# A decoder trunk in f32: the opening's products reordered, and one chunk with P3 ahead of P6

## The chip, the cores and the metric

The kernel runs on one core of a Trainium2 chip. The metric is the device time of one execution in microseconds. Engines are named as in the profile: PE is TensorE (PEld its weight loads), DVE is VectorE, ACT is ScalarE, POOL is GpSimd and SP is SyncE. POOL and SP issue the loads here.

## The reference

The input x has 512 tokens of width 1024 in float32. The trunk has two layers. Each is a half-weighted SwiGLU feed-forward part, a token mixer, and a second feed-forward part; all three read a normed h.

```python
def swiglu(x, w_in, w_out):
    g, u = jnp.split(x @ w_in, 2, axis=-1)
    return (jax.nn.silu(g) * u) @ w_out

for i in range(2):
    h = h + 0.5 * swiglu(rms_norm(h, ffn1_norm[i]), ffn1_w_in[i], ffn1_w_out[i])   # D_FF = 2816
    h = h + mixer_i(rms_norm(h, mix_norm[i]))     # layer 0: RG-LRU, layer 1: spatial gating
    h = h + 0.5 * swiglu(rms_norm(h, ffn2_norm[i]), ffn2_w_in[i], ffn2_w_out[i])
return rms_norm(h, final_norm)
```

The change touches only the start of the first feed-forward part.

## The kernel before

**Products in three parts.** Every f32 operand is split into a rounded hi part and the rest, lo. A product is three matmuls: hi by hi, hi by lo, lo by hi. For a weight tile ("raw", 512 KB) ScalarE writes whi and VectorE writes wlo; activations get hi and lo in the same way (`split`, `Group.parts`). There are four buffers each for whi and wlo, so a split waits until PE is through with the sub-step four places back. There are eight raw buffers.

**Sub-steps.** The program is one list, `subs`. A sub-step is twelve matmuls on one weight tile. The loop at the end of the kernel walks the list; in each turn it runs hooks of the phases pre, mid, rest, end and late, splits the weights of sub-steps up to three places ahead (`SPLIT_AHEAD`; the first turns have their own numbers in `ahead`), issues loads while a raw buffer is free, and writes the sub-step's products. Each engine carries out its instructions in the order in which this loop writes them. So an instruction that waits holds up all that is behind it on its engine.

**The opening.** The first 256 columns of the feed-forward part (`pair_plain`, `first=True`) are computed by plain blocks. The normed x is taken as quarters A11, A12, A22, A21 (tokens in halves by columns in halves); each quarter is loaded, transposed by PE, copied out of PSUM with the norm's gain, and split. The list is: A12 by two tiles; A11 and S1 by two tiles, S1 = A21 - A22 being multiplied by the tile that A11 has just used; and A22 by two tiles, for which VectorE adds the A12 tile to the A11 tile. The transposes stand behind the first two steps. The row scale `rt` (from squares, a root and a Newton step) is applied after the product, as the gate activation's scale.

**A chunk.** All other parts of x @ w_in and the output products use seven block products in place of eight (`seven`). For one chunk each of the seven, P1, P2, P5, P6, P3, P7, Q4 in this order, is two sub-steps (groups 0 and 1 of the inner dimension). The left sides are given by `LEFT`: P6 uses S2, P3 uses S4. The right sides come out of few tiles:

- P5 uses tile 11 after VectorE has added tile 12 to it (`Sub.add`). Then POOL issues an accumulating load that adds block 22 to tile 12, which P7 will use.
- P6 uses tile 11 after VectorE has added tile 22 to it; then an accumulating load adds block 21 to tile 11, which Q4 will use.
- P3 uses tile 22 as it was loaded.

**Banks.** `BANK` says where a product is summed. P1 starts bank A, P2 bank B, P5 bank C. P6, P7 and Q4 add to A, and P3 adds to C. Each intermediate sum is read out before the next product is added: in `chunk` a function per product does this, for the two token tiles s. `p5` copies C to c5 on ScalarE. `p6` copies A to c2, and `p3` subtracts that copy from C and multiplies by the gate c1: the result c is transposed by PE (`left_blocks`, line 260) at the end of P7's first step. A product that adds to a bank waits until the bank's last read-out is done.

Lines in the profile: L87 is every VectorE tensor_tensor, L96 every ScalarE activation, L260 the transposes, L345 to L347 a chunk's matmuls, L692 to L694 those of the opening, L136 the accumulating loads.

Of the kernel before, what the change touches and what calls it, by code (L numbers as in the profile page):

```python
# [10 lines left out]
AF = mybir.ActivationFunctionType  # L11
ALU = mybir.AluOpType

P = 128
D = 1024
T = 512
H = T // 2
# [26 lines left out]


ORDER = ("P1", "P2", "P5", "P6", "P3", "P7", "Q4")
LEFT = {"P1": "A11", "P2": "A12", "P5": "S1", "P6": "S2", "P3": "S4", "P7": "S3", "Q4": "A22"}
BANK = {"P1": ("A", True), "P2": ("B", True), "P5": ("C", True), "P6": ("A", False), "P3": ("C", False),
        "P7": ("A", False), "Q4": ("A", False)}
# [3 lines left out]
def trunk(ctx: ExitStack, tc: tile.TileContext, a: dict, out: bass.AP):  # L53
# [41 lines left out]
    def act(o, x, f, **k):  # L95
        nc.scalar.activation(out=o, in_=x, func=f, **k)  # L96
# [218 lines left out]
            return [p[:, o : o + P] for p in g.hl[LEFT[prod]]]  # L315
        return left

    def seven(block, cuts, left, w, posts, order=None, own=False, apart=False, joined=None):

        bk, raw, held = {}, {}, []
        banks = dict(BANK, Q4=("Q", True)) if apart else BANK

        def mm_of(prod, ci):
            name, fresh = banks[prod]
            pairs = cuts[ci]

            def mm(sub):
                if fresh and ci == 0:
                    for s in range(2):
                        bk[name, s] = bank(name)[:, :w]
                if prod == joined and ci == 0:
                    held.extend((sub, q, i) for q, i in enumerate(pairs))
                    return
                for s in range(2):
                    ps = bk[name, s]
                    k = {} if fresh else dict(skip_group_check=True)  # L340
                    for sb, q, i in (held if prod == joined else []) + [(sub, q, i) for q, i in enumerate(pairs)]:
                        zh, zl = left(prod, i, s)
                        wh, wl = sb.hi[:, q, :], sb.lo[:, q, :]
                        end = i == cuts[-1][-1]
                        nc.tensor.matmul(ps, zh, wh, start=fresh and i == 0, stop=False, **k)  # L345
                        nc.tensor.matmul(ps, zl, wh, start=False, stop=False, **k)  # L346
                        nc.tensor.matmul(ps, zh, wl, start=False, stop=end, **k)  # L347
# [273 lines left out]
        return left_of(lambda: S.z)  # L621


    def chunk(w_in, f0, nt, group):

        w = nt * P
        c1, c2, c3, c5, ht = {}, {}, {}, {}, {}
# [4 lines left out]
        def new(d, s, name):  # L632
            d[s] = slot(name=name)[:, :w]
            return d[s]
# [25 lines left out]
        def q4(s, ps):  # L660
# [4 lines left out]
            if s == 1:  # L665
                left_blocks(group, ht, 1)

        seven(in_block(w_in, lambda n: n * DFF + f0 * P, w), [[0, 1], [2, 3]], x_left(), w,
              dict(P1=p1, P2=p2, P5=p5, P6=p6, P3=p3, P7=p7, Q4=q4))

    def pair_plain(w_in, f0, group, first=False):

# [10 lines left out]
                st[half, s] = bank("p")  # L683
            return st[half, s]

        def product(sub, half, left, h, start, stop):
            for s in range(2):
                ps = bank_of(half, s)
                for q in range(2):
                    zh, zl = (p[:, q * H + s * P : q * H + (s + 1) * P] for p in S.z[h].hl[left])  # L690
                    wh, wl = sub.hi[:, q, :], sub.lo[:, q, :]
                    nc.tensor.matmul(ps, zh, wh, start=start and q == 0, stop=False)  # L692
                    nc.tensor.matmul(ps, zl, wh, start=False, stop=False)  # L693
                    nc.tensor.matmul(ps, zh, wl, start=False, stop=stop and q == 1)  # L694

        def post(half):
            for s in range(2):
# [5 lines left out]
            left_blocks(group, ht, half, 3 if first and half else 2)  # L703

        for h in range(2):
            subs.append(Sub(raw[1, h], lambda sub, h=h: product(sub, 0, "A12", h, h == 0, False)))
        for h in range(2):
            subs.append(Sub(raw[0, h], lambda sub, h=h: (product(sub, 0, "A11", h, False, h == 1),
                                                         product(sub, 1, "S1", h, h == 0, False)),
                            None if h == 0 else (lambda: hook(now[0] + 1, "rest", lambda: post(0))) if first else  # L710
                            lambda: post(0)))
# [553 lines left out]
    def load_more(n=len(raws)):  # L1265
        nonlocal loaded
        while loaded < n and len(live) < RAW_BUFS:
            raws[loaded].load()
            loaded += 1

    raws[0].halves = True
    load_x(0, 512, 256)
    load_x(0, 768, 256)
    load_more(2)
    load_x(0, 0)
    load_x(2, 512)
    load_x(2, 0)
    load_more()
# [34 lines left out]
        if parts:  # L1313
            first.g[i].parts("S1" if name == "A21" else name)

    opening = {}
    def take_plain(i, name):

        g, ps = first.g[i], opening.pop((i, name))
        t = g.new(name)  # L1320
        for q, gain in enumerate(first.src(i, name)[1]):
            qs = slice(q * H, (q + 1) * H)
            ts(t[:, qs], ps[:, qs], gain, None, ALU.mult)

    turn(0, "A12")
    warm_up(2, 512)
# [27 lines left out]
    hook(100, "rest", lambda: list(consts))  # L1354
    ahead = {0: 1, 1: 3, 2: 4, 3: 6}

    for i, s in enumerate(subs):
        now[0] = i
# [1 line left out]
        run("pre")  # L1360
        upto = ahead.get(i, i + SPLIT_AHEAD)
        for q in range(i, min(upto + 1, len(subs))):
            if i >= 2 and q == upto and q + 1 < len(subs):
                subs[q + 1].add()
            subs[q].split()
        run("mid")
# [33 lines left out]
```

## Time and profile before

| | |
|---|---|
| median of 3 runs | 1653.03 us (1652.65 to 1653.19) |
| profiled execution | 1654.62 us, span 1652.9 us |
| PE busy | 1624.5 us (98%) |
| DVE, ACT, POOL busy | 1373.8 (83%), 1034.6 (63%), 210.5 us (13%) |
| granted TensorE clock, mean | 0.993 |
| loads on POOL's queue | 86.06 MB, 31.1% of 16 engines' span |
| loads on SP's queue | 181.95 MB, 36.0% |

A line of the timeline has the start, the duration (of one instruction, or of a run of xN), engine, line, operation, output and inputs, shape, count and, in brackets, the engine's idle time just before and what ended it. Buffer numbers are left out of names: A, B, C are banks, whi and wlo a weight's parts, hi and lo an activation's, raw a loaded tile, e a transposed block, s in the first 80 us mostly S1. A row of the stretches has the busy time of each engine with its count, then the granted clock, the DMA engines' share, and GB/s.

### The profile page before, as it was taken

How to read it: one execution, taken by the hardware profiler on the slowest of the kernel's cores; microseconds unless marked ns; L12 is line 12 of the kernel's file. 1: busy time of each engine (PE TensorE's matmuls, PEld its weight loads, DVE VectorE, ACT ScalarE, POOL GpSimd, SP SyncE). 2: the span in 40 equal slices, each digit the busy share in tenths (PEclk: the TensorE clock that was granted, in tenths of full speed). 3: DMA queues.
4: the chain of work that ended last, by engine and by line, in shares of the span. 5: the costliest groups of instructions: out<-in, count | busy, mean ns of one | idle time of the engine just before them, and what ended most of it. 6: DMA issues, size and time to landing. Idle time of an engine off the chain costs nothing.

```text
span 1652.9 us, 20807 instructions
## 1 busy us (share of the span) xinstructions
PE 1624.5 (98%) x7475; PEld 1336.9 (81%) x7475; DVE 1373.8 (83%) x1825; ACT 1034.6 (63%) x1487; POOL 210.5 (13%) x191
## 2 busy tenths in 40 slices
PE   8999999989999999999999999999999999999996
PEld 6788888878878888888888888888888888888885
DVE  5898897786798897887988978878966988879777
ACT  6656656666867656556676565566874765665655
POOL 1111111200010111111101111111200011121110
PEclk9999999999999999999999999999999999999998
DMA  6767876952463866976838778768863557696683
GB/s 205 158 174 175 208 165 153 218 140 77 102 148 92 195 164 162 217 182 155 203 96 182 173 163 208 185 161 202 218 172 90 151 119 188 166 209 168 157 206 77
DMA packets 160744, 271.97 MB, mean 165 GB/s; under 512 B 11280, under 2 KB 37504, under 8 KB 160640
## 3 DMA queue, kind: packets, MB, share of 16 engines
q1 hardware_dynamic: 113424, 181.95, 36.0%
q0 software_dynamic: 44992, 86.06, 31.1%
q10 hardware_dynamic: 2224, 2.63, 0.5%
q8 instruction: 59, 0.97, 0.2%
q14 instruction: 45, 0.37, 0.1%
HBM read 268.50 MB, written 2.10 MB: 164 GB/s over the span
## 4 chain that ended last, share of the span: by engine, by line
PE 86%; DVE 8%; ACT 4%; issue 2%; DMA 1%; SPq 0%; ACTq 0%; DVEq 0%
PE A L346 13%; PE A L347 13%; PE A L345 13%; PE C L346 7%; PE C L347 7%; PE C L345 7%; PE B L345 3%; PE B L347 3%; PE B L346 3%; PE e L260 3%; DVE wlo L87 2%; PE p L694 1%; PE p L692 1%; PE p L693 1%; PE Q L347 1%
## 5 line engine op out<-in xcount | busy, mean ns | idle before, releaser
L96 ACT ACTIVATE whi<-raw 128x1024 fp32r<-128x1024 f32 (+1 forms) x539 | 556.4, 1034 | 421.4 <-PE A L346 107.4
L87 DVE TENSOR_TENSOR wlo<-raw,whi 128x1024 fp32r<-128x1024 f32 (+1 forms) x539 | 640.5, 1191 | 198.3 <-ACT whi L96 197.4
L345 PE MATMUL A<-whi,hi 128*128 128x512 f32 x984 | 393.0, 399 | 0.0
L346 PE MATMUL A<-whi,lo 128*128 128x512 f32 x984 | 385.5, 392 | 2.5 <-DVE lo L87 2.4
L347 PE MATMUL A<-wlo,hi 128*128 128x512 f32 x984 | 385.5, 392 | 0.2 <-DVE wlo L87 0.2
L346 PEld LDWEIGHTS A<-whi,lo 128*128 128x128 f32 x984 | 185.8, 189 | 41.7 <-DVE lo L87 4.8
L347 PEld LDWEIGHTS A<-wlo,hi 128*128 128x128 f32 x984 | 185.4, 188 | 40.8 <-DVE wlo L87 0.6
L345 PEld LDWEIGHTS A<-whi,hi 128*128 128x128 f32 x984 | 185.7, 189 | 36.5
L346 PE MATMUL C<-whi,lo 128*128 128x512 f32 x544 | 212.4, 390 | 0.9 <-DVE lo L87 0.7
L345 PE MATMUL C<-whi,hi 128*128 128x512 f32 x544 | 212.3, 390 | 0.0
L347 PE MATMUL C<-wlo,hi 128*128 128x512 f32 x544 | 211.8, 389 | 0.0
L136 POOL DMA_DIRECT2D raw<-in_ffn_w_in_dram x80 | 96.4, 1205 | 757.4 <-DVE raw L87 591.2
L87 DVE TENSOR_TENSOR raw<-raw,raw 128x1024 f32<-128x1024 f32 (+1 forms) x118 | 141.6, 1200 | 0.5
L87 DVE TENSOR_TENSOR lo<-a,hi 128x512 fp32r<-128x512 f32 (+1 forms) x196 | 127.8, 659 | 11.2 <-ACT hi L96 10.9
L136 POOL DMA_DIRECT2D raw<-in_ffn_w_out_dram x72 | 83.0, 1153 | 385.0 <-DMA raw<-in_ffn_w_out_dram 137.0
L346 PEld LDWEIGHTS C<-whi,lo 128*128 128x128 f32 x544 | 102.1, 188 | 24.1 <-DVE lo L87 3.2
L96 ACT ACTIVATE hi<-a 128x512 fp32r<-128x512 f32 (+1 forms) x196 | 117.4, 601 | 6.2 <-DVE a L87 4.0
L345 PEld LDWEIGHTS C<-whi,hi 128*128 128x128 f32 x544 | 102.1, 188 | 21.5 <-ACT c L96 0.4
L347 PEld LDWEIGHTS C<-wlo,hi 128*128 128x128 f32 x544 | 102.1, 188 | 21.0
L96 ACT ACTIVATE c<-A 128x512 f32<-128x512 f32 x126 | 74.1, 595 | 56.6 <-PE A L347 56.2
L345 PE MATMUL B<-whi,hi 128*128 128x512 f32 x272 | 109.2, 401 | 0.0
L347 PE MATMUL B<-wlo,hi 128*128 128x512 f32 x272 | 106.3, 391 | 0.0
(165 smaller groups left out, 2193.4 us busy)
## 6 DMA issues: line engine op xcount, KB each, us to landing
raw<-in_ffn_w_in_dram SPq DMA_DIRECT2D x160, 512.0 KB, 4.5
raw<-in_ffn_w_out_dram SPq DMA_DIRECT2D x100, 512.0 KB, 5.4
raw<-in_ffn_w_in_dram POOLq DMA_DIRECT2D x80, 512.0 KB, 7.6
raw<-in_ffn_w_out_dram POOLq DMA_DIRECT2D x60, 512.0 KB, 7.9
raw<-in_sg_w_in_dram SPq DMA_DIRECT2D x18, 512.0 KB, 5.0
raw<-in_rec_w_in_dram SPq DMA_DIRECT2D x16, 512.0 KB, 3.9
raw<-in_ffn_w_in_dram SPq DMA_DIRECT2D x30, 256.0 KB, 3.9
raw<-in_ffn_w_out_dram SPq DMA_DIRECT2D x20, 256.0 KB, 4.1
```

Source lines behind the costliest of these rows:

```text
L87: nc.vector.tensor_tensor(out=o, in0=x, in1=y, op=op)
L96: nc.scalar.activation(out=o, in_=x, func=f, **k)
L136: nc.gpsimd.dma_start(out=self.v, in_=src, accum_op=ALU.add)
L260: nc.tensor.transpose(ps[:, o : o + P], src(q, s), ident)
L345: nc.tensor.matmul(ps, zh, wh, start=fresh and i == 0, stop=False, **k)
L346: nc.tensor.matmul(ps, zl, wh, start=False, stop=False, **k)
L347: nc.tensor.matmul(ps, zh, wl, start=False, stop=end, **k)
L692: nc.tensor.matmul(ps, zh, wh, start=start and q == 0, stop=False)
L693: nc.tensor.matmul(ps, zl, wh, start=False, stop=False)
L694: nc.tensor.matmul(ps, zh, wl, start=False, stop=stop and q == 1)
```

## The change

In the opening A11's two steps come before S1's two (which use the same split tiles again), three matmul kinds go around over the four blocks of a tile (all hi by hi first), the transposes stand inside steps, after the eighth matmul, half of A11's copy out of PSUM goes to VectorE, and the tiles for A11 are loaded ahead of the second half of x. The list is two steps longer, each with less in it.

In the first chunk (`late`) the order is P1, P2, P5, P3, P6, P7, Q4. Tile 11 gets block 22 by an accumulating load after P5's split, not by VectorE, so two VectorE adds are gone and two loads of 512 KB on POOL's queue are new; tile 22 is used by P3 alone. For the two orders one function `p36` serves both products: the first copies its bank, the second subtracts.

```diff
+LATE = ("P1", "P2", "P5", "P3", "P6", "P7", "Q4")
...
-        order = order or [(p, ci) for p in ORDER for ci in range(len(cuts))]
+        order = order or [(p, ci) for p in (LATE if late else ORDER) for ci in range(len(cuts))]
...
                 r = raw[11, ci]
+                if late:
+                    then = block(1, 1, cuts[ci])
+            elif prod == "P6" and late:
+                r, then = raw[11, ci], block(1, 0, cuts[ci])
+            elif prod == "P3" and late:
+                r = new(1, 1)
             elif prod == "P6":
...
-        def p6(s, ps):
-            act(new(c2, s, "c2"), ps, AF.Copy)
-
-        def p3(s, ps):
-            tt(c2[s], ps, c2[s], ALU.subtract)
+        def p36(s, ps):
+            if s not in c2:
+                act(new(c2, s, "c2"), ps, AF.Copy)
+                return
+            tt(c2[s], *((c2[s], ps) if late else (ps, c2[s])), ALU.subtract)
             stt(c2[s], c2[s], rt(s), c1[s], ALU.mult, ALU.mult)
...
+            sq = [(s, q) for s in range(2) for q in range(2)]
+            for i, (s, q, m) in enumerate([(s, q, m) for m in range(3) for s, q in sq] if first else
+                                          [(s, q, m) for s, q in sq for m in range(3)]):
+                if i == 8 and between is not None:
+                    between()
...
+                                                                opening["A11"] if first and h else None)))
+        if first:
+            for h in range(2):
+                subs.append(Sub(raw[0, h], lambda sub, h=h: product(sub, 0, "A11", h, False, h == 1,
+                                                                    opening["A21"] if h else None)))
+            for h in range(2):
+                subs.append(Again(subs[2 + h], lambda sub, h=h: product(sub, 1, "S1", h, h == 0, False),
+                                  None if h == 0 else lambda: hook(now[0] + 1, "rest", lambda: post(0))))
...
-                    chunk(w_in, f0, n, groups[-1])
+                    chunk(w_in, f0, n, groups[-1], f0 == 2 and len(subs) < 20)
...
     load_x(0, 0)
+    load_more(4)
     load_x(2, 512)
     load_x(2, 0)
...
+    def take_a11(i):
+        take_plain(i, "A11", (1,))
+        first.g[i].parts("A11")
+        subs[2 + i].split()
...
-    for n, phase, fn in ((0, "end", lambda: (turn(0, "A11"), turn(1, "A11"))),
-                         (0, "end", lambda: (turn(0, "A22", bank), turn(1, "A22", bank))),
-                         (0, "late", vec_rest),
-                         (1, "pre", lambda: (take(0, "A11"), take_plain(0, "A22"), take_plain(1, "A22"))),
-                         (1, "pre", lambda: (subs[2].split(), take(1, "A11"))),
-                         (1, "end", lambda: (turn(0, "A21"), turn(1, "A21"))),
-                         (2, "pre", lambda: (take(0, "A21", False), take(1, "A21", False))),
-                         (2, "pre", lambda: [g.parts("S1") for g in first.g]),
-                         (3, "pre", lambda: [g.parts("A22") for g in first.g])):
+    for name in ("A11", "A21"):
+        opening[name] = lambda name=name: (turn(0, name), turn(1, name))
+    for n, phase, fn in ((0, "late", vec_rest),
+                         (2, "pre", lambda: (take_a11(0), take_a11(1))),
+                         (2, "end", lambda: (turn(0, "A22", bank), turn(1, "A22", bank))),
+                         (3, "mid", lambda: (take_plain(0, "A22"), take_plain(1, "A22"))),
+                         (4, "pre", lambda: (take(0, "A21", False), first.g[0].parts("S1"))),
+                         (4, "pre", lambda: (take(1, "A21", False), first.g[1].parts("S1"))),
+                         (5, "pre", lambda: [g.parts("A22") for g in first.g])):
         hook(n, phase, fn)
-    squares(2, "mid", "A11")
-    squares(2, "mid", "A12")
-    squares(3, "mid", "A22")
-    squares(3, "mid", "A21")
-    rstd(3, (0, "late"), (0, "late"), (1, "pre"))
-    first.rest(1, None)
+    squares(3, "mid", "A11")
+    squares(3, "mid", "A12")
+    squares(4, "mid", "A22")
+    squares(5, "mid", "A21")
+    rstd(5, (0, "mid"), (0, "mid"), (0, "rest"))
+    first.rest(3, None)
...
-    ahead = {0: 1, 1: 3, 2: 4, 3: 6}
+    ahead = {0: 1, 1: 1, 2: 3, 3: 3, 4: 6, 5: 7}
```

More of the change, by code (lines that the diff above doesn't have):

```diff
@@ L316, in left_of, with seven @@
         return left
-    def seven(block, cuts, left, w, posts, order=None, own=False, apart=False, joined=None):
+    def seven(block, cuts, left, w, posts, order=None, own=False, apart=False, joined=None, late=False):
         bk, raw, held = {}, {}, []
@@ L621, in x_left, with chunk @@
         return left_of(lambda: S.z)
-    def chunk(w_in, f0, nt, group):
+    def chunk(w_in, f0, nt, group, late):
         w = nt * P
@@ L668, in chunk @@
         seven(in_block(w_in, lambda n: n * DFF + f0 * P, w), [[0, 1], [2, 3]], x_left(), w,
-              dict(P1=p1, P2=p2, P5=p5, P6=p6, P3=p3, P7=p7, Q4=q4))
+              dict(P1=p1, P2=p2, P5=p5, P6=p36, P3=p36, P7=p7, Q4=q4), late=late)
     def pair_plain(w_in, f0, group, first=False):
@@ L684, in bank_of, with product @@
             return st[half, s]
[L686 to L694, printed above, removed]
+        def product(sub, half, left, h, start, stop, between=None):
+            sq = [(s, q) for s in range(2) for q in range(2)]
[3 more added lines that the diff above has]
+                    between()
+                z = S.z[h].hl[left][m == 1][:, q * H + s * P : q * H + (s + 1) * P]
+                nc.tensor.matmul(bank_of(half, s), z, (sub.lo if m == 2 else sub.hi)[:, q, :],
+                                 start=start and q == 0 and m == 0, stop=stop and q == 1 and m == 2)
         def post(half):
@@ L705, in pair_plain @@
         for h in range(2):
-            subs.append(Sub(raw[1, h], lambda sub, h=h: product(sub, 0, "A12", h, h == 0, False)))
-        for h in range(2):
+            subs.append(Sub(raw[1, h], lambda sub, h=h: product(sub, 0, "A12", h, h == 0, False,
+                                                                opening["A11"] if first and h else None)))
[6 more added lines that the diff above has]
+                                  None if h == 0 else lambda: hook(now[0] + 1, "rest", lambda: post(0))))
+        for h in () if first else range(2):
             subs.append(Sub(raw[0, h], lambda sub, h=h: (product(sub, 0, "A11", h, False, h == 1),
                                                          product(sub, 1, "S1", h, h == 0, False)),
-                            None if h == 0 else (lambda: hook(now[0] + 1, "rest", lambda: post(0))) if first else
-                            lambda: post(0)))
+                            None if h == 0 else lambda: post(0)))
         for h in range(2):
@@ L1269, in load_more @@
             loaded += 1
+    opening = {}
     raws[0].halves = True
@@ L1314, in take, with take_plain @@
             first.g[i].parts("S1" if name == "A21" else name)
-    opening = {}
-    def take_plain(i, name):
+    def take_plain(i, name, qs=(0, 1)):
         g, ps = first.g[i], opening.pop((i, name))
@@ L1321, in take_plain @@
         for q, gain in enumerate(first.src(i, name)[1]):
-            qs = slice(q * H, (q + 1) * H)
-            ts(t[:, qs], ps[:, qs], gain, None, ALU.mult)
+            c = slice(q * H, (q + 1) * H)
+            if q in qs:
+                ts(t[:, c], ps[:, c], gain, None, ALU.mult)
+            else:
+                act(t[:, c], ps[:, c], AF.Copy, scale=gain)
+    def take_a11(i):
+        take_plain(i, "A11", (1,))
+        first.g[i].parts("A11")
+        subs[2 + i].split()
     turn(0, "A12")
@@ L1362, in trunk @@
         for q in range(i, min(upto + 1, len(subs))):
-            if i >= 2 and q == upto and q + 1 < len(subs):
+            if i >= 4 and q == upto and q + 1 < len(subs):
                 subs[q + 1].add()
```

## The prediction

> **What bounds the kernel now.** I read the page's busy shares first, then TensorE's own timeline for its idle places, then, for each place, the engine that is named there.
>
> ```profile
> PE 1624.5 (98%) x7475; PEld 1336.9 (81%) x7475; DVE 1373.8 (83%) x1825; ACT 1034.6 (63%) x1487; POOL 210.5 (13%) x191
> 12.70 1.07 PE L260 MATMUL e<-ident,x 128*128 128x128 f32 x8 [2.00 <-DMA x<-in_x_dram]
> 55.79 0.39 PE L345 MATMUL A<-whi,hi 128*128 128x512 f32 x1
> 61.84 0.50 PE L345 MATMUL C<-whi,hi 128*128 128x512 f32 x1
> 62.17 0.39 PE L346 MATMUL C<-whi,lo 128*128 128x512 f32 x1
> 69.91 0.39 PE L347 MATMUL A<-wlo,hi 128*128 128x512 f32 x1
> 72.50 0.90 PE L260 MATMUL e<-ident,c 128*128 128x128 f32 x3 [1.00 <-DVE c L93]
> 75.33 0.63 PE L347 MATMUL A<-wlo,hi 128*128 128x512 f32 x1
> 77.22 0.60 PE L260 MATMUL e<-ident,c 128*128 128x128 f32 x4
> ```
>
> TensorE is full: of 1652.9 us only 28 are idle, so an edit of the first 80 us can gain no more than what is lost there. A product takes (69.91 - 62.17)/34 = 0.228 us from start to start, a step of twelve 2.73 us, a transpose 1.07/8 = 0.13 us. Two places lose time. Before 12.70 TensorE waits for x. And P7's first step ends at 69.91 + 0.23 = 70.1, but the transposes that follow wait for the gate tile c until 72.50. With them (0.5) and P7's second step (2.7) the row at 77.22 would stand at 73.4: 3.8 us are lost. Part of that is the clock:
>
> ```profile
> 11.06:14.47 3.41, 1.49 (x12) 1.00 1.05 365
> 69.08:72.50 3.42, 1.52 (x8) 1.00 0.77 232
> 72.50:75.91 3.41, 3.41 (x10) 0.50 0.77 123
> 362.63:366.05 3.42, 1.13 (x8) 1.00 0.22 66
> 461.62:465.03 3.41, 1.24 (x6) 1.00 0.95 196
> ```
>
> These are stretches of 3.413 us on one grid: length, PE busy, granted clock. A stretch with 1.1 to 1.5 us of work is followed by one at half clock, as the row of 72.50 shows, where a product takes 0.43 us or nearly twice as long. Each costs up to 1.7 us. The last two rows are the other places of so little work, later on.
>
> Why c is late shows on VectorE, which is busy without a pause in this part (5.00 of 5.00 us in the first row, the third pair of figures):
>
> ```profile
> 50.00:55.00 5.00, 5.00 (x25) 4.09 (x23) 5.00 (x6) 2.53 (x5) 0.00 (x0) 1.00 1.10 210
> 39.86 0.88 DVE L93 SCALAR_TENSOR_TENSOR h<-p,rt,s 128x256 f32<-128x256 f32 x2 [0.57 <-ACT s L96]
> 47.78 1.22 DVE L87 TENSOR_TENSOR wlo<-raw,whi 128x1024 fp32r<-128x1024 f32 x1
> 50.46 1.22 DVE L87 TENSOR_TENSOR raw<-raw,raw 128x1024 f32<-128x1024 f32 x1
> 51.59 1.22 DVE L87 TENSOR_TENSOR wlo<-raw,whi 128x1024 fp32r<-128x1024 f32 x1
> 53.07 1.22 DVE L87 TENSOR_TENSOR raw<-raw,raw 128x1024 f32<-128x1024 f32 x1
> 57.74 0.42 DVE L87 TENSOR_TENSOR s<-e,a 128x256 f32<-128x256 f32 x1
> 69.58 0.69 DVE L87 TENSOR_TENSOR c<-C,c 128x512 f32<-128x512 f32 x1
> ```
>
> **The opening.** It keeps its 96 products and 32 transposes. Eight products of the second A12 step move into the idle time before 12.70 (1.8 us), and A11's transposes follow them. What comes then is held by ScalarE and VectorE, not by the products.
>
> ```profile
> 13.37 0.84 ACT L96 ACTIVATE a<-e,vec 128x256 f32<-128x256 f32 x2 [2.83 <-PE e L260]
> 21.32 1.65 DVE L93 SCALAR_TENSOR_TENSOR s<-e,vec,a 128x256 f32<-128x256 f32 x4
> 24.28 2.35 DVE L87 TENSOR_TENSOR raw<-raw,raw 128x1024 f32<-128x1024 f32 x2
> L96 ACT ACTIVATE junk<-x x8: 615/617/617, 27.6 to 34.9; 128x512 f32<-128x512 f32 x8
> 30.08 1.14 ACT L96 ACTIVATE hi<-a 128x512 fp32r<-128x512 f32 x2
> 35.60 0.16 DVE L87 TENSOR_TENSOR ti<-ss 128x4 f32<-128x4 f32 x1 [1.04 <-ACT junk L96]
> ```
>
> A11's first copy starts at 13.37 as before. Two halves (0.84), the split's hi (0.53 to the next start) and the first weight's whi (1.06) put A11's first products at 15.9. The second group's copy has one half on VectorE behind wlo of the first weight (1.22), so the second weight is ready only at 19.05. Products, A22's transposes (1.07) and then A21's lead to S1 at 23.7, where before it stood at 23.0 but with twelve products fewer behind it. So TensorE is 2 us ahead here. It gives that back: A21's transposes let VectorE begin S1 at 22.2, and S1's two tiles go one after the other: two gains (0.8 by the row at 21.32), then the split's hi on ScalarE and lo behind it (about 1.3 together), twice. The two adds for A22 so start at 26.3 instead of 24.28. From these adds to A22's hi were 30.08 - 24.28 = 5.8 us with four squares between; now two squares stand there (1.2 less), which gives 30.9 against 30.08, and A22's products start near 31.6, where they were at 31.7. From that hi to ti were 35.60 - 30.08 = 5.5 us with a P1 split (0.97 of whi) and two squares that now stand elsewhere: 3.3, and ti comes at 34.2 to 34.3. From ti to h were 39.86 - 35.60 = 4.3; P1's first whi now stands there too, and h starts at about 39.5. I take 0.4 us earlier for VectorE's chain; ends are 1 earlier and 0.8 later (if loads land later in their new order). For TensorE the opening ends between 0.1 earlier and 1 later, as A22's new wait of 2.4 us may halve the clock. TensorE's end does not enter the sum, because of what follows.
>
> **The first chunk.** Removed: two VectorE adds (50.46 and 53.07), 1.13 us each to the next start, so all behind them on VectorE is 2.3 + 0.4 = 2.7 us earlier. That alone would take away the wait at 72.50. Added: two loads of 512 KB on POOL's queue. Moved: P3 to right behind P5. In the program P3 adds to bank C, which P5's copy c<-C must have read, and ScalarE takes its instructions in order: gate activation c, whi of the sub-step three ahead, hi of S4's second half, then c<-C.
>
> ```profile
> 58.19 0.42 ACT L96 ACTIVATE hi<-s 128x256 fp32r<-128x256 f32 x1 [2.75 <-DVE s L87]
> 58.51 1.32 ACT L96 ACTIVATE c<-c,rt 128x512 f32<-128x512 f32 x2
> 59.74 1.04 ACT L96 ACTIVATE whi<-raw 128x1024 fp32r<-128x1024 f32 x1
> 60.69 0.62 ACT L96 ACTIVATE hi<-a 128x512 fp32r<-128x512 f32 x1
> 61.21 1.06 ACT L96 ACTIVATE c<-C 128x512 f32<-128x512 f32 x2
> 61.84 0.19 PEld L345 LDWEIGHTS C<-whi,hi 128*128 128x128 f32 x1 [0.36 <-ACT c L96]
> ```
>
> Already before, P3 at 61.84 waited 0.36 us for this copy, though P6's two steps stood in between. Now P3 wants to start at 55.8, and the copy hangs on VectorE's s (57.74) through hi. So P3 cannot start before 61.84 - 2.7 = 59.1, even if nothing else is late: a stall of 3.3 us that VectorE's gain does not reach.
>
> Something else is late. The whi ahead of the copy is now P6's, and its tile is the one that the added load fills after P5's split.
>
> ```profile
> 45.59 1.28 POOL L136 DMA_DIRECT2D raw<-in_ffn_w_in_dram  x1 [39.39 <-DVE raw L87]
> 48.18 1.21 POOL L136 DMA_DIRECT2D raw<-in_ffn_w_in_dram  x1 [1.32 <-DVE raw L87]
> 55.72 1.20 POOL L136 DMA_DIRECT2D raw<-in_ffn_w_in_dram  x1 [6.33 <-DVE wlo L87]
> raw<-in_ffn_w_in_dram POOLq DMA_DIRECT2D x1, 512.0 KB, 8.3
> raw<-in_ffn_w_in_dram POOLq DMA_DIRECT2D x1, 512.0 KB, 6.0
> q0 software_dynamic: 109, 0.20, 112.5%
> ```
>
> The landings are those of the second and third issue; the last row is the queue from 53 to 54 us. The second lands at 48.18 + 8.3 = 56.5, or 56.1 when 0.4 us earlier. The new load is issued after P5's wlo (47.78 + 1.22 - 0.4 = 48.6) and after POOL's issue before it, at 49.05, and stands third in the queue. At 0.20 MB per us its 0.52 MB takes 2.6 us more: 58.7, and some 0.5 us for a w_out load that P3's freed tile now lets in: 59.2. Ends: 6.0 us from its issue, 55.1, which leaves the bound of 59.1 above in charge; and 60.7, if that w_out traffic takes its full share. From the landing, whi (0.97 to the next start), hi (0.52) and the first copy (0.6) put P3 at 59.2 + 2.2 = 61.4.
>
> The idle time is then 5.6 us. On the grid (69.08 less 3.413 each) the stretch 58.84 to 62.26 holds 0.9 us of work, so the clock stays half until 65.67: 4.3 us at half speed, 2.1 lost. POOL's next add to the same tile follows P6's split and lands near 67.6, before Q4's whi needs it. P7 now adds to bank A right behind P6; VectorE's subtraction that reads it (0.7) stands behind Q4's whi and wlo (2.2), whose buffers P6's first step frees: up to 3.2 us with the hand-overs against 2.73 for P6's second step, so 0.5 us. Sum to the row at 77.22: P3's start 61.4, six steps 16.4, transposes 0.5, this wait 0.5, clock 2.1: 80.9. That is 3.7 us later. The rest of the kernel has TensorE full and moves with it. Against the profiled execution (1654.6 us, with 1.7 around its span; the median of the runs is 1653.03) this gives 1658.3, against the median 1656.7. From landings between 58.6 and 60.7 P3 starts between 60.8 and 62.9, the clock loses 2.4 to 1.4, and the sum is 3.4 to 4.5 us later.
>
> The Trainium skill's page DMA: Bandwidth & Descriptors (Anatomy of one DMA, SWDGE path) gives 2.0 us plus bytes over 436 GB/s, an estimate of 3.2 us here. The measured 6.0 and 8.3 disagree and decide; by the page P3 would start at 59.1.
>
> **Rivals.** *Landing in time* (chance 0.11): the copy alone sets P3 at 59.1; the clock is back at 62.26, 1.6 lost: 59.1 + 16.4 + 1.0 + 1.6 = 78.1, 0.9 later, 1653.9. For it: 6.0 us for a load alone. Against: two loads stand ahead.
> *No halving* (0.08): a partly used stretch keeps the clock; 3.7 - 2.1 = 1.6 later, 1654.6. Against it: stretches with 1.52 and 1.49 us of work halved it. This is what the Trainium skill's TensorE: Matmul & The Clock Gate (Part 1: The HAM clock gate) would make of it, as it asks for an idle window of 3.4 us; the row of 69.08 speaks against that.
> *Later halvings go* (0.13): the shift moves the idle times near 364 and 464 us on the grid so that one or both fall on two stretches; each gives back 1.7: 3.7 less 1.7 or 3.4, 1653.3 to 1655.0. At 3.7 us, nearly one grid step, they mostly stay.
> *Queue worse* (0.16): four loads with the w_out loads among them land up to 2.5 us later; 5 to 7 later, 1658 to 1660.
> *Faster* (0.10): the copy is made before P3 wants it, and the wait at 72.50 is gone too: 55.8 + 16.4 + 1.0 = 73.2, 4 us less, 1649.0. This needs P6's whi off ScalarE by 54.5, so a landing 4.5 us after the issue, below every POOL row of 512 KB here, and s on VectorE 4 us earlier.
>
> **How the numbers follow.** The forecast has 0.42. About 0.2% (3.3 us) is what a measurement of this kernel can tell from no change. Slower by more: the forecast less a small part of it, and the worse queue, 0.55. Within: three rivals and that small part, 0.35. Faster: 0.10. The range from 1652.8 to 1659.5 leaves out the faster rival and the end of the worse queue. The forecast's own range is 1656.4 to 1657.5.
>
> **What would show it.** Right: TensorE idle for about 5 us before P3's first product on C, released by ScalarE's c; whi ahead of it waiting for a DMA; half clock after it; no wait for c at the transposes behind P7; A22's first products in the opening waiting for hi. Wrong: P3 following P5 without a gap, the added load landing by 54 us, or an idle place that I have not named beyond 80 us.

## The result, and the profile after

| | before | after |
|---|---|---|
| median of 6 runs | 1653.14 us (1652.65 to 1654.51) | 1660.60 us (1659.97 to 1661.16) |
| ratio | | 1.0045, 95% interval 1.0035 to 1.0056 |
| profiled execution | 1654.62 us, span 1652.9 | 1660.58 us, span 1658.9 |

The changed kernel is slower by 7.5 us by the medians and by 6.0 us between the two profiled executions. The forecast was 3.7 us and the range ended at 1659.5: the sign was right, the size was not.

In the profile of the changed kernel the line numbers are a little higher: L97 is every ScalarE activation, L88 and L94 VectorE, L137 the accumulating loads, L347 to L349 a chunk's matmuls, L261 the transposes, L702 the opening's matmuls. First the page's busy shares, and the group of P3's and P5's products, with its idle time before them in the last columns:

```profile
PE 1624.0 (98%) x7475; PEld 1336.3 (81%) x7475; DVE 1373.0 (83%) x1825; ACT 1034.1 (62%) x1485; POOL 212.2 (13%) x193
L347 PE MATMUL C<-whi,hi 128*128 128x512 f32 x544 | 213.3, 392 | 5.8 <-ACT c L97 5.8
```

TensorE does the same work as before (1624.0 against 1624.5 us busy). All the new idle time of this group is one wait of 5.8 us for ScalarE's copy c. TensorE's timeline shows the place:

```profile
62.65 0.80 PE L347 MATMUL C<-whi,hi 128*128 128x512 f32 x1 [5.77 <-ACT c L97]
76.07 0.47 PE L347 MATMUL A<-whi,hi 128*128 128x512 f32 x1 [0.20 <-DVE c L88]
78.90 0.60 PE L261 MATMUL e<-ident,c 128*128 128x128 f32 x4
82.11 0.60 PE L261 MATMUL e<-ident,c 128*128 128x128 f32 x4
```

The first row is P3's first product, the second P7's; the last two are the transposes of the gate tile c. They wait for nothing now. Before they waited 1.00 us in the row at 72.50 that the prediction shows, and 0.91 us in the row ahead of it:

```profile
71.20 0.30 PE L260 MATMUL e<-ident,c 128*128 128x128 f32 x1 [0.91 <-DVE c L93]
```

But the row at 82.11, which answers to the one of before at 77.22, is 4.9 us later. ScalarE's timeline tells why P3 waits:

```profile
56.08 0.42 ACT L97 ACTIVATE hi<-s 128x256 fp32r<-128x256 f32 x1 [3.18 <-DVE s L88]
56.40 1.32 ACT L97 ACTIVATE c<-c,rt 128x512 f32<-128x512 f32 x2
60.53 1.06 ACT L97 ACTIVATE whi<-raw 128x1024 fp32r<-128x1024 f32 x1 [2.81 <-DMA raw<-in_ffn_w_in_dram]
61.50 0.61 ACT L97 ACTIVATE hi<-a 128x512 fp32r<-128x512 f32 x1
62.02 1.06 ACT L97 ACTIVATE c<-C 128x512 f32<-128x512 f32 x2
```

The copy c<-C stands fifth in this row of instructions. The third, P6's whi, waits 2.81 us for the added load, although P3 does not need that weight. The loads' issues on POOL's timeline (the second row is two issues):

```profile
45.74 1.28 POOL L137 DMA_DIRECT2D raw<-in_ffn_w_in_dram  x1 [39.57 <-DMA raw<-in_ffn_w_out_dram]
48.34 2.44 POOL L137 DMA_DIRECT2D raw<-in_ffn_w_in_dram  x2 [1.31 <-DVE raw L88]
52.14 1.19 POOL L137 DMA_DIRECT2D raw<-in_ffn_w_in_dram  x1 [1.37 <-DVE wlo L88]
```

And in the table of issues, where the last figure is us from issue to landing; the rows are the first issue, the second, the second and third together, and the fourth:

```profile
raw<-in_ffn_w_in_dram POOLq DMA_DIRECT2D x1, 512.0 KB, 8.8
raw<-in_ffn_w_in_dram POOLq DMA_DIRECT2D x1, 512.0 KB, 9.3
raw<-in_ffn_w_in_dram POOLq DMA_DIRECT2D x2, 512.0 KB, 10.1
raw<-in_ffn_w_in_dram POOLq DMA_DIRECT2D x1, 512.0 KB, 11.6
```

The third issue begins some 1.25 us after 48.34, at 49.6. With 9.3 for the second and a median of 10.1 for both, the third takes 10.9 us: it lands at 60.5, where whi starts.

The wait also halves the clock. In the stretches of the clock's grid (length, busy time of PE, PEld, DVE, ACT and POOL with counts, granted clock, DMA share, GB/s):

```profile
56.80:60.20 3.40, 0.08 (x1) 0.00 (x0) 1.65 (x4) 0.92 (x2) 0.00 (x0) 1.00 1.12 239
60.20:63.60 3.40, 0.95 (x2) 0.83 (x3) 1.98 (x3) 2.54 (x4) 0.45 (x1) 0.50 0.88 238
63.60:67.03 3.43, 3.43 (x9) 2.64 (x8) 2.95 (x5) 1.58 (x2) 1.38 (x2) 0.50 0.56 72
```

P3 starts at 62.65 and runs at half clock until 67.03: 4.4 us at half speed, 2.2 lost.

### The profile page after: what moved, and what is told of

Its sections match the earlier page's. It is cut to its first block, busy times and chain, and to the rows that moved or that the text cites. A ratio compares the mean times of both kernels' runs of the same rounds, so it can differ in the third digit from the quotient of the medians.

```text
span 1658.9 us, 20805 instructions
## 1 busy us (share of the span) xinstructions
PE 1624.0 (98%) x7475; PEld 1336.3 (81%) x7475; DVE 1373.0 (83%) x1825; ACT 1034.1 (62%) x1485; POOL 212.2 (13%) x193
## 4 chain that ended last, share of the span: by engine, by line
PE 85%; DVE 8%; ACT 4%; issue 2%; DMA 1%; SPq 0%; POOL 0%; ACTq 0%; DVEq 0%; POOLq 0%
PE A L348 13%; PE A L347 13%; PE A L349 13%; PE C L348 7%; PE C L349 7%; PE C L347 7%; PE p L702 5%; PE e L261 3%; PE B L347 3%; PE B L349 3%; PE B L348 3%; DVE wlo L88 2%; PE Q L347 1%; PE Q L349 1%; PE Q L348 1%
## 5 line engine op out<-in xcount | busy, mean ns | idle before, releaser
L97 ACT ACTIVATE whi<-raw 128x1024 fp32r<-128x1024 f32 (+1 forms) x539 | 556.6, 1034 | 427.1 <-PE A L348 110.4
L88 DVE TENSOR_TENSOR wlo<-raw,whi 128x1024 fp32r<-128x1024 f32 (+1 forms) x539 | 641.5, 1192 | 205.5 <-ACT whi L97 204.7
L347 PE MATMUL A<-whi,hi 128*128 128x512 f32 x984 | 392.3, 399 | 0.2 <-DVE c L88 0.2
L349 PE MATMUL A<-wlo,hi 128*128 128x512 f32 x984 | 384.8, 391 | 0.0
L347 PE MATMUL C<-whi,hi 128*128 128x512 f32 x544 | 213.3, 392 | 5.8 <-ACT c L97 5.8
L349 PEld LDWEIGHTS A<-wlo,hi 128*128 128x128 f32 x984 | 185.2, 188 | 40.1
L347 PEld LDWEIGHTS A<-whi,hi 128*128 128x128 f32 x984 | 185.1, 188 | 37.0 <-issue 0.6
L349 PE MATMUL C<-wlo,hi 128*128 128x512 f32 x544 | 212.6, 391 | 0.0
L137 POOL DMA_DIRECT2D raw<-in_ffn_w_in_dram x82 | 98.8, 1206 | 760.9 <-DVE raw L88 552.2
L88 DVE TENSOR_TENSOR raw<-raw,raw 128x1024 f32<-128x1024 f32 (+1 forms) x116 | 139.2, 1201 | 0.5
L88 DVE TENSOR_TENSOR lo<-a,hi 128x512 fp32r<-128x512 f32 (+1 forms) x196 | 128.1, 660 | 8.2 <-ACT hi L97 7.8
L137 POOL DMA_DIRECT2D raw<-in_ffn_w_out_dram x72 | 83.0, 1153 | 384.0 <-DVE wlo L88 140.4
L347 PEld LDWEIGHTS C<-whi,hi 128*128 128x128 f32 x544 | 102.7, 189 | 27.5 <-ACT c L97 6.2
L97 ACT ACTIVATE hi<-a 128x512 fp32r<-128x512 f32 (+1 forms) x196 | 117.4, 601 | 8.1 <-DVE a L88 4.0
L349 PEld LDWEIGHTS C<-wlo,hi 128*128 128x128 f32 x544 | 102.5, 188 | 21.4
L347 PE MATMUL B<-whi,hi 128*128 128x512 f32 x272 | 109.1, 401 | 0.0
L97 ACT ACTIVATE c<-A 128x512 f32<-128x512 f32 x124 | 73.0, 594 | 55.4 <-PE A L349 54.9
L349 PE MATMUL B<-wlo,hi 128*128 128x512 f32 x272 | 106.2, 390 | 0.0
```

The source lines that it names most:

```text
L88: nc.vector.tensor_tensor(out=o, in0=x, in1=y, op=op)
L137: nc.gpsimd.dma_start(out=self.v, in_=src, accum_op=ALU.add)
```

## The experiments

Each result is the median, with the lowest and highest run, and the ratio to the kernel before on the same chip with its 95% interval. Line numbers differ a little from kernel to kernel; the operations and names tell the rows apart.

**The chunk alone.** The opening of before, with the late chunk (`late` and all that hangs on it).

> The opening of before with the new first chunk (P3 ahead of P6, the accumulating load after P5's split). Theory 1, the stall at P3: it hangs on ScalarE's c<-C, which stands behind P6's whi, which waits for the third load on POOL's queue; VectorE's chain, which sets the issue of that load, was only 0.2 us later in the changed kernel, so P3 starts again near 62.5 us and the time stays within 1 us of the changed kernel: 1659.5 to 1661. Theory 2, the opening costs (TensorE reached P1 at 39.35 instead of 37.17 us there): without it the time falls to before or below it, 1649 to 1655.

Measured: 1659.44 us (1658.07 to 1659.81), ratio 1.0042 (1.0028 to 1.0056). Most of the loss is here: 6.6 us against 1652.83 for before in the same comparison. The time is just under the first theory's range, and P3 starts 1.2 us earlier than in the changed kernel, though its wait is longer:

```profile
61.43 0.79 PE L346 MATMUL C<-whi,hi 128*128 128x512 f32 x1 [6.64 <-ACT c L97]
```

POOL issues the third load 1.3 us earlier in this execution (48.3), and by the same reading as above it takes 11.0 us to land.

**The opening alone.**

```diff
-                    chunk(w_in, f0, n, groups[-1], f0 == 2 and len(subs) < 20)
+                    chunk(w_in, f0, n, groups[-1], False)
```

> The new opening with the first chunk of before (order P5, P6, P3; VectorE adds tile 22). Theory 1: TensorE's 2.2 us at P1 are taken up by the wait for c at the transposes behind P7, which VectorE sets 0.2 us later than before; as the idle time there is shorter, the clock may stay full: 1651.5 to 1654. Theory 2: the opening's loss stays in the sum: 1655 to 1661.

Measured: 1653.38 us (1651.56 to 1655.37), ratio 1.0003 (0.9994 to 1.0012). The opening costs nothing that can be told from no change. The waits for c (0.89 and 1.00 us in this trace) stand as before. So what happens on TensorE in the opening is absorbed there.

**One split moved, so that the copy goes first.** In the changed kernel P6's first split is made a turn later; the copy of C then stands ahead of its whi on ScalarE.

```diff
-    ahead = {0: 1, 1: 1, 2: 3, 3: 3, 4: 6, 5: 7}
+    ahead = {0: 1, 1: 1, 2: 3, 3: 3, 4: 6, 5: 7, 13: 15}
```

> The changed kernel, but in the turn of P5's second step the weights are split only two places ahead, so that P6's whi stands behind c<-C on ScalarE. Theory 1: P3 waits no more for the load, only for VectorE's s through the gate activations, and starts near 58.9 instead of 62.65 us; P6 does not need its load before 64. 3.8 us off P3's start and 0.6 to 2.2 off the half clock: 1654.5 to 1656.5. Theory 3, the shared bank alone (any product that adds to C right behind P5 stalls like this): 1659 to 1661, P3 near 62.

Measured: 1655.87 us (1654.67 to 1656.63), ratio 1.0021 (1.0012 to 1.0030). TensorE's timeline, with VectorE's at the second wait:

```profile
58.59 0.50 PE L347 MATMUL C<-whi,hi 128*128 128x512 f32 x1 [2.66 <-ACT c L97]
72.56 0.47 PE L347 MATMUL A<-whi,hi 128*128 128x512 f32 x1 [2.79 <-DVE c L88]
69.45 2.36 DVE L88 TENSOR_TENSOR wlo<-raw,whi 128x1024 fp32r<-128x1024 f32 x2
71.73 0.68 DVE L88 TENSOR_TENSOR c<-c,A 128x512 f32<-128x512 f32 x1
```

P3 starts 4.1 us earlier, and its wait falls from 5.77 to 2.66 us (the clock stayed full behind A22's wait in the opening here, so TensorE also came to P3 earlier). What no longer stands ahead of the copy is P6's whi, with its wait for the load (2.81 us) and its own time (0.97 us to the next start). But 2.79 us come back at P7. It adds to bank A, which VectorE's subtraction reads, and two wlo (2.3 us) stand ahead of that subtraction.

**The order alone.** P3 ahead of P6, but tile 22 is added to tile 11 by VectorE, as before: no added load.

```diff
-                if late:
-                    then = block(1, 1, cuts[ci])
             elif prod == "P6" and late:
-                r, then = raw[11, ci], block(1, 0, cuts[ci])
+                r, tile, then = raw[11, ci], raw[22, ci], block(1, 0, cuts[ci])
             elif prod == "P3" and late:
-                r = new(1, 1)
+                r = raw[22, ci] = new(1, 1)
```

> The changed kernel with P3 ahead of P6, but without the added load: VectorE adds tile 22 for P6, as before, now behind its s. Theory 1: P6's whi is ready near 57.3 us, c<-C follows at 58.7 and P3 starts near 59.4: 3.2 us off P3's start, about 0.6 off the half clock, 1656 to 1658. Theory 3, the order alone makes the stall: 1659 to 1661. If the load alone made it, P3 would follow P5 without a gap and the time would be 1653 or below.

Measured: 1656.45 us (1655.50 to 1657.73), ratio 1.0026 (1.0017 to 1.0036).

```profile
59.32 0.78 PE L347 MATMUL C<-whi,hi 128*128 128x512 f32 x1 [2.90 <-ACT c L97]
```

So the order loses 3.6 us against before in the same comparison (1652.83) and 3.1 us against the opening alone (1653.38), with no load to wait for: P3 adds to the bank that P5 has just filled, and its copy comes 2.9 us too late.

**Two splits moved.** As with one, and Q4's first split a turn later too, behind the subtraction.

```diff
-    ahead = {0: 1, 1: 1, 2: 3, 3: 3, 4: 6, 5: 7}
+    ahead = {0: 1, 1: 1, 2: 3, 3: 3, 4: 6, 5: 7, 13: 15, 17: 19}
```

> The changed kernel with two splits put one turn later: P6's (as in the run with one split moved, so that the copy of C stands ahead of it on ScalarE) and Q4's first, so that VectorE's subtraction that reads bank A stands ahead of Q4's wlo. Theory (each stall is an engine's order with a late accumulating load in it): P3's first product at 58.6 us as there, P7's wait of 2.8 us falls to 1.7 or less, the rest of it being the second late load: 1654 to 1655.5 us. Rival (P7 waits for something else than the instructions queued ahead of the subtraction): the wait stays at 2.8 us and the time at 1655.9.

Measured: 1655.03 us (1653.22 to 1657.71), ratio 1.0012 (1.0003 to 1.0021).

```profile
58.24 0.79 PE L347 MATMUL C<-whi,hi 128*128 128x512 f32 x1 [2.71 <-ACT c L97]
70.68 0.39 PE L347 MATMUL A<-whi,hi 128*128 128x512 f32 x1
69.54 0.68 DVE L88 TENSOR_TENSOR c<-c,A 128x512 f32<-128x512 f32 x1
```

P7 (the second row) waits for nothing: the subtraction ends at 70.22, where with one split moved it ended at 72.41. Not all of this is the split. The second late load also landed 1.1 us earlier (P6's second whi, which waits for it, starts at 63.39 instead of 64.45). And the clock was at half from P3's start to 61.26, which the run with one split moved did not have; by that 1.5 us TensorE came to P7 later. At full clock P7 would have waited some 1.2 us (an estimate from these rows), within the forecast of 1.7 us or less. The median is 0.8 us lower, though the two intervals overlap. What is left is P3's 2.7 us and the half clock behind it.

**A bank of its own for P3.** The two splits moved, and P3 summed in a fresh bank D; VectorE adds D to P5's copy.

```diff
+        banks = dict(BANK, P3=("D", True)) if late else BANK
...
-                act(new(c2, s, "c2"), ps, AF.Copy)
+                tt(new(c2, s, "c2"), c5[s], ps, ALU.add)
```

> The same two splits, and P3 summed in a fresh bank D of its own (VectorE adds D to P5's copy in place of ScalarE's copy of C), so that P3 needs not wait for the read-out of C. Theory (the order costs because P3 adds to the bank that P5 has just filled): P3 follows P5 without a gap, at 55.8 to 56.7 us; but P6 then wants its tile 2 to 3 us earlier and waits for the accumulating load's landing near 60 to 61 us, so that the time is 1653.5 to 1655.5 us, near that of the kernel before and not below it. Rival (bank and read-out cost little, the load is all): time as with the two splits alone, within 0.5 us.

Measured: 1656.48 us (1655.77 to 1657.52), ratio 1.0026 (1.0016 to 1.0035): a miss by 1 us.

```profile
71.79 0.47 PE L347 MATMUL A<-whi,hi 128*128 128x512 f32 x1 [3.15 <-DVE c L88]
68.64 1.28 DVE L88 TENSOR_TENSOR c<-c,D 128x512 f32<-128x512 f32 x2
69.83 1.22 DVE L88 TENSOR_TENSOR wlo<-raw,whi 128x1024 fp32r<-128x1024 f32 x1
70.97 0.68 DVE L88 TENSOR_TENSOR c<-c,A 128x512 f32<-128x512 f32 x1
```

P3 follows P5 without a gap, as forecast. But the 3 us come back at P7; P6, where the theory had them, loses 0.7 us in two waits for wlo. The addition of D (1.19 us to the next start) and a wlo (1.14) now stand ahead of the subtraction that frees bank A. The same chunk behind the opening of before gives the next result.

> The opening of the kernel before, with the chunk in the new order, the accumulating load, the two splits a turn later and P3 in a bank of its own. Theory (loads limit, the opening adds nothing to a chunk that waits for loads): within 1 us of the run with own bank and new opening, 1653 to 1655.5 us. Rival (the new opening costs by itself once the wait for c no longer absorbs it): 1 to 2 us faster than that run.

Measured: 1655.41 us (1654.38 to 1659.00), ratio 1.0019 (1.0010 to 1.0028), with the same wait of 3.14 us at P7. It lies 1.1 us under the run with the new opening, between the two expectations, and the intervals overlap: inconclusive.

**The same without the load.** Own bank, two splits moved, VectorE's addition in place of the load.

> The changed kernel with VectorE's addition in place of the accumulating load (as in the run with the order alone), the two splits a turn later and P3 in a bank of its own: neither the load nor the bank makes anything wait. Theory: P3 follows P5, P6 follows P3, c is made while P6 runs, no wait stands at the transposes behind P7's first step, and the row that answers to the one of before at 77.22 us stands at 74.5 to 75.5: 1650.5 to 1652 us, faster than the kernel before. Rival (VectorE, with the two additions back, is late with something else by as much): a new wait of 2 us or more within the chunk, 1653 to 1655 us.

Measured: 1655.76 us (1654.64 to 1657.08), ratio 1.0022 (1.0013 to 1.0031). The theory missed. The rival's new wait is there, with a time 0.8 us above the rival's range:

```profile
71.13 0.47 PE L347 MATMUL A<-whi,hi 128*128 128x512 f32 x1 [3.03 <-ACT whi L97]
67.97 1.28 DVE L88 TENSOR_TENSOR c<-c,D 128x512 f32<-128x512 f32 x2
69.16 1.22 DVE L88 TENSOR_TENSOR wlo<-raw,whi 128x1024 fp32r<-128x1024 f32 x1
70.30 0.68 DVE L88 TENSOR_TENSOR c<-c,A 128x512 f32<-128x512 f32 x1
```

The bracket names whi, but P7's own whi started at 64.54 and 66.01; the one that ends close to P7's start is Q4's. The subtraction ends at 70.98 and P7 starts 0.15 us later, as in the run before (71.65 and 0.14). So the rows point to VectorE once more. Neither the bank nor the load makes P3 wait here, and the chunk still loses 2.7 us. The rows suggest that VectorE is behind, and that whatever of TensorE first needs its newest result pays.

**The kernel before, with only the order of the splits changed.** If that is so, the chunk of before needs no new product order, only its splits out of the way of c. (A split is ScalarE's whi as well as VectorE's wlo; the wait at the transposes is for VectorE's c.)

```diff
-    ahead = {0: 1, 1: 3, 2: 4, 3: 6}
+    ahead = {0: 1, 1: 3, 2: 4, 3: 6, 15: 17}
```

> The kernel before, with nothing but one split put a turn later: Q4's first, so that its wlo (1.13 us) stands behind the four VectorE instructions that make the gate tile c. Theory (what the chunk loses is VectorE's order, not its load of work): c is made 1.1 us earlier, the waits at the transposes behind P7's first step (0.91 and 1.00 us) come to about 0.8 together, and the half clock behind them goes in most executions: 1651 to 1652.3 us. Rival (VectorE is simply full, so that work put off there is missed again at once): a wait of about 1 us for Q4's wlo comes in its place, 1652.5 to 1653.5 us.

Measured: 1651.34 us (1649.75 to 1652.88), ratio 0.9990 (0.9981 to 0.9999). Of the two waits for c one is left, and no half clock follows it:

```profile
70.86 0.55 PE L260 MATMUL e<-ident,c 128*128 128x128 f32 x3 [0.91 <-DVE c L93]
```

Then with `14: 16, 15: 16` in place of `15: 17`:

> The kernel before, with P7's second split put two turns later and Q4's first one turn later: both wlo (2.3 us) stand behind the gate tile c. Theory: c is there when P7's first step ends (waits of 0 to 0.3 us), then a wait of 0.1 to 0.5 us for P7's second wlo, no half clock in this place: 1650.5 to 1651.8 us, faster than both kernels. Rival (VectorE is full): the wait for P7's second wlo is 1 us or more, 1652 to 1653.5 us.

Measured: 1650.10 us (1648.88 to 1652.97), ratio 0.9984 (0.9975 to 0.9993): the lowest median of all, 3 us under before in the same comparison, and about 10 under the changed kernel's median. Its interval overlaps with that of the run with one split.

```profile
67.85 0.68 DVE L87 TENSOR_TENSOR c<-C,c 128x512 f32<-128x512 f32 x1
70.62 4.09 DVE L87 TENSOR_TENSOR wlo<-raw,whi 128x1024 fp32r<-128x1024 f32 x4
70.67 0.64 PE L260 MATMUL e<-ident,c 128*128 128x128 f32 x4
71.90 0.50 PE L347 MATMUL A<-wlo,hi 128*128 128x512 f32 x1
74.30 0.60 PE L260 MATMUL e<-ident,c 128*128 128x128 f32 x4
```

c starts at 67.85 instead of 69.58, and the four wlo come behind it. The transposes wait for nothing; the one price is P7's second wlo, 0.3 us late at 71.90 (0.52 from the product before it, where 0.23 is the pace). The last row stands 2.9 us ahead of the one of before at 77.22. The waits make 1.6 us of this (0.91 and 1.00, less 0.3); the rest fits the half clock of before's execution behind them. The new opening with the same two splits:

> The opening of the changed kernel, the chunk of the kernel before, and the same two splits put later. With the wait for c gone, nothing behind the opening absorbs what the opening gains or costs. Theory from the opening's rows (A22's products wait 2.3 us for hi, some executions at half clock behind it, so that TensorE enters the chunk up to 2 us later in those, and 0.3 to 0.6 us later otherwise): 0.3 to 1.5 us slower than the kernel before with the same two splits. Rival (VectorE's chain sets the chunk all the same): within 0.3 us of it.

Measured: 1651.34 us (1649.61 to 1652.84), ratio 0.9988 (0.9980 to 0.9997). It is 1.2 us slower than with the old opening, as the theory had it, but the intervals overlap: whether the opening costs anything when nothing absorbs it stays open.

## Why the prediction was wrong

**The mechanism was right.** P3 waits for ScalarE's copy behind P6's whi behind the third load: the rows at 60.53 to 62.65 are the ones that the prediction named, and P3 starts 4.1 us earlier in the run in which this whi stands behind the copy. From the landing to P3 it had 2.2 us and 2.1 were measured, from P3 to the row of the transposes 19.5 and 19.46. P7's wait for bank A had 0.5 and took 0.20. The bound by the copy alone (59.1) is near what remains without the load (59.32).

**One agreement is luck.** At half clock 2.1 us were forecast as lost and 2.2 measured. But the prediction laid the grid of before's execution over the changed kernel, with the half clock ending at 65.67. The changed kernel's execution has another grid: the half clock ends at 67.03, 1.36 us later, and P3 starts 1.25 us later. The two errors cancel; on the assumed grid a start at 62.65 would have lost 1.5 us.

**The step that failed is the landing of the third load: 59.2 forecast, 60.5 measured.** It makes the 1.2 us that the transposes are later than forecast. More than half of it is the queue: 10.9 us from issue to landing, where the forecast's 59.2 - 49.05 allowed 10.15. By the same reading the third load took 11.0 to 11.6 us in the five other runs that have the four loads, so this part does not hang on one execution. The forecast carried over 8.3 us for the second load and put the third 3.1 behind it; here the second took 9.3. Why four loads are this slow is not shown. The low end given for the landing (6.0 us from issue) was far off; the high end, 60.7, was right, and its sum, 4.5 us later, is near the measured 4.9.

The other 0.55 us is the issue, at 49.6 instead of 49.05. POOL's issues follow VectorE, whose chain was taken 0.4 us earlier; in this execution it is 0.2 later:

```profile
26.90 2.35 DVE L88 TENSOR_TENSOR raw<-raw,raw 128x1024 f32<-128x1024 f32 x2
31.48 1.14 ACT L97 ACTIVATE hi<-a 128x512 fp32r<-128x512 f32 x2
34.82 0.16 DVE L88 TENSOR_TENSOR ti<-ss 128x4 f32<-128x4 f32 x1
40.03 0.88 DVE L94 SCALAR_TENSOR_TENSOR h<-p,rt,s 128x256 f32<-128x256 f32 x2 [0.38 <-ACT s L97]
```

The adds were expected at 26.3, A22's hi at 30.9, ti at 34.2 to 34.3 and h at 39.5: each is 0.5 to 0.6 late, so the chain from the adds on was right. The delay comes from before the adds, and it is no steady cost of the new opening. S1 starts at 22.54 instead of 22.2 already. And in the run with two splits moved, which has the same opening, h starts at 39.49 and the loads are issued as forecast (the row is the second and the third issue, so the third is at 49.05):

```profile
47.80 2.44 POOL L137 DMA_DIRECT2D raw<-in_ffn_w_in_dram  x2 [1.32 <-DVE raw L88]
```

There, too, P6's whi waits for the load until 60.05. Over the traces h starts between 39.40 and 40.12 with the new opening and between 38.74 and 40.40 with the old one, so 0.6 us between two executions says little about the opening.

**Then two terms that the sum did not have.** Two places of TensorE's timeline, in the profiled execution of before and then of after:

```profile
364.63 0.33 PE L495 MATMUL xt<-ident,xn 128*128 128x128 f32 x1 [2.12 <-ACT xn L96]
1635.45 0.50 PE L346 MATMUL Q<-whi,lo 128*128 128x512 f32 x1 [0.30 <-DVE lo L87]
```

```profile
369.90 0.33 PE L503 MATMUL xt<-ident,xn 128*128 128x128 f32 x1 [2.13 <-ACT xn L97]
1641.40 0.50 PE L348 MATMUL Q<-whi,lo 128*128 128x512 f32 x1 [0.29 <-DVE lo L88]
```

The delay is 4.9 us at the transposes, 5.3 at the first pair and 5.95 at the second. "The rest moves with it" missed 1.0 us, spread over 1550 us in steps of about 0.3 us or less, for which no cause was found.

Last, the profiled execution of before is 1.5 us above its median, and that of the changed kernel is at its median. The forecast carried the difference of the profiled executions over to the medians. Before's execution had the half clock at 72.50 (1.7 us), and the change was credited with its going. The mean granted clocks bear on this. Before's profiled execution has 0.993, with four stretches at half clock ahead of its last products (they begin at 14.47, 72.50, 366.05 and 465.03); that of the run with one split moved in the kernel before has 0.997 and none. So each such stretch lowers the mean by some 0.001. The 82 other executions of before in the experiments have a median of 0.995: some two halved stretches fewer than the profiled one. That the one at 72.50 is among those missing is argued, not shown, as the clocks by stretch are on record for profiled executions only. The terms add up: 3.7 + 1.2 + 1.0 + 1.5 = 7.4. Of the three that the forecast lacked, this last one is the largest.

**The opening.** TensorE's wait for A22 was forecast as 2.4 us, perhaps with a half clock: it is 2.28, and the half clock came. The timeline's row, and the two stretches around it (the granted clock is the third figure from the end):

```profile
32.15 1.47 PE L702 MATMUL p<-whi,hi 128*128 128x512 f32 x4 [2.28 <-ACT hi L97]
```

```profile
29.50:32.91 3.41, 1.13 (x5) 0.67 (x4) 2.01 (x3) 3.41 (x8) 0.00 (x0) 0.99 0.98 308
32.91:36.33 3.42, 3.42 (x9) 2.67 (x8) 2.07 (x4) 3.39 (x8) 0.00 (x0) 0.51 0.55 153
```

In the run with two splits moved, which has the same opening, the clock stayed full behind a wait of 2.27 us. Again the timeline's row and the two stretches around it; the half clock behind P3 from 57.84 to 61.26 gives that execution's grid, in steps of 3.413 us:

```profile
31.59 1.19 PE L702 MATMUL p<-whi,hi 128*128 128x512 f32 x4 [2.27 <-ACT hi L97]
```

```profile
27.13:30.54 3.41, 2.19 (x10) 1.49 (x8) 2.28 (x3) 1.80 (x4) 0.00 (x0) 1.00 0.48 151
30.54:33.95 3.41, 2.35 (x10) 1.97 (x11) 2.71 (x4) 3.41 (x8) 0.00 (x0) 1.00 0.87 262
```

Here the wait lies across an edge of the grid, so that neither stretch is left with little work.

That its end does not enter the sum was right: the run of the opening alone is at 1.0003.

**The rivals.** A landing in time, no halving and the faster case did not happen, and the later halvings stayed (the waits at 369.90 and 470.0 are still there, with half clock behind each). What came is nearest in size to the worse queue, which had 0.16, 5 to 7 us and an end at 1660, 0.6 us under the median; of its 2.5 us later landing 1.3 were seen. So the size is that rival's, but only in part for its reason. The faster case failed for a reason beyond the one given. With its own bank and no load P3 waits 0.4 us at most (for an activation's lo), and the chunk is still no faster, since P7 then waits for VectorE.

## What to carry to other kernels

When TensorE waits for a chain on a full engine, look first at what stands ahead of the chain in that engine's order and is not yet needed. Two weight splits written behind the gate tile brought 3 us, where a new product order with 2.3 us less work for that engine lost 7.5. A product that is moved to right behind the one that fills its bank is bound by that bank's read-out, and every instruction written ahead of the read-out, with whatever each waits for, joins the path. A forecast made against one profiled execution should say which of its losses the median execution has; the mean granted clocks of the runs give a first hint.

## What the runs showed of the hardware

Four accumulating loads of 512 KB issued on POOL's queue within 6.4 us landed after 8.8, 9.3, 10.9 and 11.6 us, where in the kernel before one issued 7.5 us behind the last took 6.0. Of the four each further one took longer. SP's loads of w_out used the DMA engines in part of the same time; how much of the delay is theirs was not tried.

The same gap of TensorE is followed by half clock in one execution and not in another, since it falls differently on the stretches: the two waits of 2.28 and 2.27 us above. The stretch with 1.13 us of work was followed by half clock, those with 2.19 and 2.35 us were not. The Trainium skill's page TensorE: Matmul & The Clock Gate (Part 1: The HAM clock gate) says that the activity window of 3.4 us runs free and does not start with the kernel; the two rows agree. It puts the low clock behind an idle window. Here a stretch with 1.13 of 3.41 us of work was already followed by half clock, so a window need not be wholly idle.
